# A two-layer encoder on one core: halves of x in two loads each, squares on two engines, constant products around the first norm, later places for means between the layers

## The chip, the cores and the metric

The kernel runs on one core of one Trainium2 chip. The metric is the device time of one execution in microseconds (us), the median of several runs. A core has a matrix engine (TensorE, PE in the profile; PEld is its loading of the stationary operand), a vector engine (VectorE, DVE), an engine for functions of one operand (ScalarE, ACT), a general one (GpSimd, POOL) and one that only issues transfers (SyncE, SP). Each works through its own queue in order and waits on semaphores. Matrix products are accumulated in PSUM, eight banks of 128 x 512 float32; everything else lies in SBUF.

## The reference

Two layers on x of 512 positions by 1024 channels, float32. All norms are RMS norms over the channels.

```
mem_n = rms_norm(mem, mem_norm_g)
for l in range(2):
    h = rms_norm(x, g_pre_mix[l])
    q_a, k_a, v_a, q_b, k_b, v_b, q_m, gate_pre = split(h @ w_in[l])
    o_a, o_b, o_m = neighbourhood(...), dilated(...), memory(q_m, mem_n @ w_mem_kv[l])
    merged = sum of sigmoid(gate_pre + b_gate[l]) * (o @ w_br)   # three branches
    x = x + rms_norm(merged @ w_out[l], g_post_mix[l])
    h = rms_norm(x, g_pre_ffn[l])
    u = depthwise_conv(h @ w_up[l], width 3)
    x = x + rms_norm((gelu(a) * b) @ w_down[l], g_post_ffn[l])   # a, b: halves of u
```

## The kernel before

Everything is held with channels on the 128 partitions and positions along the free side: x is eight tiles (index k) of 128 channels by 512 positions, worked in two halves of 256 positions. A product of full accuracy is made of three products: each operand is split into a high part (an ACT cast) and a low part (a subtraction on DVE or POOL), and `mm3` adds high by high, high by low and low by high. Weights come in blocks of 512 KB by SP (`weights`, line 226, three buffers `wraw`) and are split in the same way.

A norm needs the sum of squares over the channels, that is over partitions. ACT squares the tiles, DVE adds some of them, and `rstd_job` (line 325) lets PE multiply the sums as the stationary operand with a column of 1/1024 (`mean`): for each accumulator and each block of 128 positions one product of one column, which the trace records twice. ACT takes the square root, DVE the reciprocal, and two PE transposes spread the result over the partitions. In what follows "a mean" is these products, "the transposes" are the two of line 341.

The order of PE's instructions is written by a planner (`Woven`, line 46). It has a clock that each PE instruction advances by a planned cost (line 250: 0.107 us for three-part products of 256 columns, 0.213 for 512), and jobs, which are generators: `yield t` makes a job due t later by that clock, and it goes on at the first `tick` after that (`run_group` and `linear` tick after each k). `need(flag)` runs jobs until the flag is given. The planner does not measure; where a job's data are late on the chip, PE stands. The order on the other engines is set at build time by a scheduler that follows the order of the program as far as operands are ready in its own reckoning.

Three places matter here.

The start: `load_x` (line 192) brings the first half of x in four transfers of two tiles. Two constant products (`idle(2)`, line 883) run on PE meanwhile. `first_squares` (line 864) squares the eight tiles on ACT and adds them in pairs on DVE, so that the first half's mean has four accumulators; the second half's are added further, to two. `pre_norm_job` (line 363) does the norm: mean, root, reciprocal, transposes, then for each k a scaling on DVE, the high part on ACT, the low part on DVE. In between stand the splits of the first layer weights. The first projections need h of the first half (flag `h0.0.0`).

Between the layers: the last linear of layer 0 (`sublayer_end` with one tile, number 7, in halves) hands each half to a job. For the first half it is `end_job` (line 378): mean and transposes of the post-norm, then for each k a product, an addition into x, a square of the new x added to `acc2`; then `yield 9.0` (line 390) and the next layer's `pre_norm_job`, whose mean reads `acc2`. The second half goes through `raw_end_job` (line 417), which makes its own mean and, after `yield 3.5` (line 435), one over the new x. During this PE does the four memory projections of the next layer (`mem_kv`, line 478, 24 products of 256 columns each, every one into a new `mmbank` tile), and then the first pair of layer 1's projections for the first half.

Between mixing and channel mixing, in both layers: `factor_end_job` (line 393), once for each half, does the post-norm, adds into x, writes the not yet normalised h for the up-projection, squares, and after `yield 3.5` (line 409) takes the mean and copies the factor R. The first four up-projections run as a group over the halves (in two `sbank`, one `obank` and one `mmbank` tile); then come linears of 24 products of 512 columns, each in an `mmbank` tile. R is first read when the projections are read out (`scaled`, line 358).

```
131    ps_mm = ctx.enter_context(tc.tile_pool(name="ps_mm", bufs=3, space=bass.MemoryType.PSUM))
846                pss = [(sbank if SB and n0 == 0 and m % 2 else mmbank)((128, 256)) for m in pair]
482            ps = mmbank((128, N_MEM))
```

So full tiles, half tiles and memory projections share three buffers, and a new one waits until an old one has been read. The functions that the diff touches, and what calls them:

Of the kernel before, what the change touches and what calls it, by code (L numbers as in the profile page):

```python
# [9 lines left out]
AF = mybir.ActivationFunctionType  # L10
# [10 lines left out]
KD = D_MODEL // 128  # L21
# [4 lines left out]
HALVES = (slice(0, 256), slice(256, 512))  # L26
# [5 lines left out]
V_PRE, V_POST, V_PREF, V_POSTF, V_BG, V_CW, V_CB = 0, 8, 16, 24, 32, 56, 188  # L32
# [87 lines left out]
def tile_hybrid_encoder(ctx, tc, xT, memT, memg, vecs, rpb, w_in, w_kv, w_bra, w_brb, w_brm,  # L120
                        w_out, w_up, w_down, c_ident, c_mask, c_tab0, c_tab1, out):
    nc = tc.nc
# [14 lines left out]
    wv = Woven(tc)  # L137
# [12 lines left out]
    def ktile(dt=F32R, shape=(128, 512)):  # L150
        return tp.tile(list(shape), dt, tag="ka", name=nm("ka"), bufs=12)

    def ytile(shape=(128, 512)):
        return tp.tile(list(shape), F32, tag="y", name=nm("y"), bufs=8)
# [4 lines left out]
    def smalls(n=2):  # L159
        return sp.tile([128, n], F32, tag="st", name=nm("st"))  # L160
# [7 lines left out]
    def tbank(shape=(128, 512)):  # L168
        return ps_t.tile(list(shape), F32, tag="pt", name=nm("pt"))

    def obank(p=64):
        return ps_o.tile([p, 512], F32, tag="o", name=nm("o"))
# [5 lines left out]
    ACT, V = Counted(nc.scalar, wv, 0.1, 0.8e-3), Counted(nc.vector, wv, 0.065, 1.05e-3)  # L178
# [8 lines left out]
    xs = const.tile([128, 2, KD, 256], F32, name="x")  # L187

    def xh(k, half):
        return xs[:, half.start // 256, k, :]  # L190

    def load_x(half):
        for k in range(0, KD, 2):
            i = half.start // 256
            nc.sync.dma_start(out=xs[:, i, k:k + 2, :], in_=xT[:, i, k:k + 2, :])

    g0 = const.tile([128, KD], F32, name="g0")
    nc.scalar.dma_start(out=g0, in_=vecs[:, 0, V_PRE:V_PRE + KD])
# [46 lines left out]
    def mm(ps, a, b, first, last, cost):  # L245
        wv.pe(nc.tensor.matmul(ps, a, b, start=first, stop=last), cost)  # L246
# [66 lines left out]
    def sumsq_add(acc, src, first, slot=None, eng=None):  # L313
        if first:
            ACT.activation(acc, src, AF.Square)
        else:
            n = acc.shape[-1]
            sq = slot((128, 256)) if slot else small("sq2", 4) if n == 256 else small("sq", 1, (128, 512))
            ACT.activation(sq, src, AF.Square)
            (eng or V).tensor_add(acc, acc, sq)  # L320
# [1 line left out]
    def acctile():  # L322
        return small("acc", 2, (128, 512))

    def rstd_job(accs, n, box):

        nb = n // 128
        bank = tbank((128, n + nb))
        pr, pt = bank[:, 0:n], bank[:, n:n + nb]
        for i, a in enumerate(accs):  # L330
            for b in range(nb):
                mm(pt[:, b:b + 1], a[:, 128 * b:128 * b + 128], mean, i == 0 and b == 0,
                   i == len(accs) - 1 and b == nb - 1, 0.11)
        rs = smalls(nb)
        crit[0] = ACT.activation(rs, pt, AF.Sqrt, bias=eps, scale=1.0).ins
        V.reciprocal(rs, rs)
        yield 0.8
        for b in range(nb):
            one = rs[:, b:b + 1]
            spread = bass.AP(one.tensor, one.offset, [list(one.ap[0]), [0, 128]])  # L340
            wv.pe(nc.tensor.transpose(pr[:, 128 * b:128 * b + 128], spread, ident), 0.11)
        box.append(pr)

    def normed(src, g, rs, hi, lo, eng=None):
        h32 = small("h32", 3)
        V.scalar_tensor_tensor(out=h32, in0=src, scalar=g, in1=rs, op0=ALU.mult, op1=ALU.mult)
        split(h32, hi, lo, eng)

    def raw_split(l, goff, k, src, hi, lo):

        g = vec[:, l, goff + k:goff + k + 1]
        ACT.activation(hi, src, AF.Copy, scale=g)
        V.scalar_tensor_tensor(out=lo, in0=src, scalar=g, in1=f32(hi), op0=ALU.mult, op1=ALU.subtract)

    def rtile():
        return tp.tile([128, 512], F32, tag="R", name=nm("R"), bufs=1)
# [3 lines left out]
        V.tensor_mul(y, ps, R)  # L360
        return y

    def pre_norm_job(l, goff, acc, hs, i):
        half, box = HALVES[i], []
        yield from rstd_job(acc if isinstance(acc, list) else [acc[:, half]], 256, box)
        for k in range(KD):
            g = g0[:, k:k + 1] if l == 0 and goff == V_PRE else vec[:, l, goff + k:goff + k + 1]
            normed(xh(k, half), g, box[0], hs[k][0][:, half], hs[k][1][:, half],
                   G if k in LOG[l > 0 and goff == V_PRE] else V)
        crit[0] = last_copy[0]  # L370
        yield 1.2
        wv.give(f"h{l}.{goff}.{i}")
# [5 lines left out]
    def end_job(l, goff, og, acc, acc2, i, then, lat, more=()):  # L378
        half, box = HALVES[i], []
        yield lat  # L380
        yield from rstd_job([acc[:, half]] + list(more), 256, box)
        for k in range(KD):
            V.tensor_mul(og[k][:, half], og[k][:, half], box[0])
            (G if then is None and i and k in TAILG else V).tensor_add(xh(k, half), xh(k, half), og[k][:, half])
            if acc2 is not None:
                sumsq_add(acc2[:, half], xh(k, half), k == 0, None, G if k in SQG[goff == V_POSTF] else V)
            else:
                nc.sync.dma_start(out=out[:, k, half], in_=xh(k, half))
        if then is not None:
            yield 9.0  # L390
            yield from then(i)

    def factor_end_job(l, goff, og, acc, acc2, i, nxt):
# [23 lines left out]
    def raw_end_job(l, goff, og, acc, acc2, nxt, lat):  # L417


        half, box = HALVES[1], []  # L420
        hs, raw, R = nxt
        yield lat
        raw.extend((t[:, 0, :], t[:, 1, :]) for t in [ktile(F32R, (128, 2, 256)) for _ in range(KD)])
        yield from rstd_job([acc[:, half]], 256, box)
        for k in range(KD):
            V.tensor_mul(og[k][:, half], og[k][:, half], box[0])
            V.tensor_add(xh(k, half), xh(k, half), og[k][:, half])
            raw_split(l + 1, V_PRE, k, xh(k, half), *raw[k])
            if k == 0:
                yield 0.6  # L430
            wv.give(f"raw{k}")
            yield 1.05
        for k in range(KD):
            sumsq_add(acc2[:, half], xh(k, half), k == 0)
        yield 3.5
        box = []
        yield from rstd_job([acc2[:, half]], 256, box)
        ACT.copy(R[:, half], box[0])
        wv.give("R")
        for k in range(KD):  # L440
            normed(xh(k, half), vec[:, l + 1, V_PRE + k:V_PRE + k + 1], box[0], hs[k][0][:, half], hs[k][1][:, half])
        crit[0] = last_copy[0]
        yield 1.2
        wv.give(f"h{l + 1}.{V_PRE}.1")

    def h_tiles():
        return [(htile(), htile()) for _ in range(KD)]
# [46 lines left out]
    def group_weights(srcs, engs):  # L494
        return [weights(s, KD, 128, big, e) for s, e in zip(srcs, engs)]
# [368 lines left out]
    def first_squares(half):  # L864
        sqs = [ytile((128, 256)) for _ in range(KD)]
        for k in range(KD):
            ACT.activation(sqs[k], xh(k, half), AF.Square)
            if k % 2:
                V.tensor_add(sqs[k], sqs[k], sqs[k - 1])
            if k in (3, 5) and half != HALVES[0]:  # L870
                V.tensor_add(sqs[k], sqs[k], sqs[k - 2])
        return sqs[1::2] if half == HALVES[0] else sqs[5::2]

    idle_bank = obank(128)

    def idle(n):

        one, none = mean[:, 0:1], zero[:, 0:1]
        a, b = (bass.AP(t.tensor, t.offset, [list(t.ap[0]), [0, w]]) for t, w in ((one, 128), (none, 512)))
        for _ in range(n):  # L880
            mm(idle_bank, a, b, True, True, 0.0)

    idle(2)
    hs = h_tiles()
    wv.spawn(pre_norm_job(0, V_PRE, first_squares(HALVES[0]), hs, 0))
    gw = group_weights([w_in[0, m] for m in FIRST[:2]], (V, V))
    load_x(HALVES[1])
    nc.sync.dma_start(out=vec, in_=vecs)
    wv.need(f"h0.{V_PRE}.0")
    with tc.issue_after(last_copy[0]):  # L890
        sqs = first_squares(HALVES[1])
    wv.spawn(pre_norm_job(0, V_PRE, sqs, hs, 1), SD1)
    gw += group_weights([w_in[0, m] for m in FIRST[2:]], (V, G, V, G))
    for t, c in ((mask, c_mask), (tab0, c_tab0), (tab1, c_tab1)):
# [5 lines left out]
    for l in range(depth):  # L900
# [29 lines left out]
        acc = [None] * KD  # L930
# [20 lines left out]
        hs, R, gw = h_tiles(), rtile(), []  # L951
# [17 lines left out]
        for j in range(NFF):  # L969
            pair = []  # L970
            for m in (j, j + NFF):
# [3 lines left out]
                w = ahead.pop()  # L975
# [24 lines left out]
        else:  # L1000
            hm, km, vm = [], [], []
            wv.spawn(mem_norm_job(l + 1, hm, htile), 20.0)
            pre, R, raw, box = [], rtile(), [], []

            def then(a, i, l=l, box=box):
                box.extend(h_tiles())
                return pre_norm_job(l + 1, V_PRE, a, box, i)
# [21 lines left out]
            hs = box  # L1029
# [93 lines left out]
```

## Time and profile before

| | us |
|---|---|
| median of 3 runs (lowest to highest) | 1555.03 (1553.63 to 1556.48) |
| the profiled execution | 1552.91 |
| its span, first to last instruction | 1550.9 |
| PE busy | 1522.6 |
| DVE busy | 948.8 |
| ACT busy | 739.7 |
| POOL busy | 148.6 |

A timeline row reads: start, duration from the first start to the last end, engine, line, operation, tile written <- tiles read, shape, number of instructions, and in brackets how long the engine was idle before and what released it. L114 is a helper that issues for ACT and DVE, L246 the one for products, so rows are told apart by their tiles: `x` the stream, `y` and `sq` squares and scratch, `acc` sums of squares, `pt` the bank of a mean, `mm`, `s`, `o` banks of products, `st` the small root, `h` and `ka` operands, `m`, `whi`, `wlo` split weights and other large tiles. "PE pt <- DVE acc" in the waits is total time, number of times, longest. A row of a table by stretches has, after the stretch and its length, busy time and instructions of PE, PEld, DVE, ACT and POOL, the granted clock of PE as a share, the share of the transfer engines and their GB/s. The profile gives a granted clock of 1.00 until its first record of the clock, also where products run at half the pace.

### The profile page before, as it was taken

What the parts mean: (1) busy time and instruction counts of PE and PEld (TensorE: products, weight loads), DVE (VectorE), ACT (ScalarE), POOL (GpSimd) and SP (SyncE); (2) the same over time, 40 slices, a digit from 0 to 9 for tenths busy, and PEclk for the clock granted to TensorE, in tenths of its full rate; (3) what the DMA queues carried; (4) which work ended last, traced back from release to release, by engine and by line L of the source; (5) the groups of instructions that cost most, each with busy time, mean ns of one, the idle gap of its engine ahead of it and who ended that gap; (6) DMA issues with size and microseconds to landing.
All of it is one profiled execution on the core that took longest, in us unless ns stands there. A gap on an engine that the chain in (4) does not pass through costs nothing.

```text
span 1550.9 us, 20677 instructions
## 1 busy us (share of the span) xinstructions
PE 1522.6 (98%) x7970; PEld 1300.1 (84%) x7970; DVE 948.8 (61%) x1684; ACT 739.7 (48%) x1288; POOL 148.6 (10%) x216
## 2 busy tenths in 40 slices
PE   8999999999999999999989999999999999999997
PEld 7988878888988888888888888888889888888887
DVE  6685666335777777743397856753456977776233
ACT  6465575235544444533355556742354544444231
POOL 3340000210000000010154300002100000000000
PEclk9999999999999999999999999999999999999998
DMA  7221113234112332333431221132350223233331
GB/s 246 91 90 61 61 57 98 93 95 157 61 55 96 99 104 96 108 96 102 129 103 59 79 69 58 52 109 88 102 177 15 82 96 98 102 99 89 98 105 62
DMA packets 45810, 144.91 MB, mean 93 GB/s; under 512 B 5376, under 2 KB 9600, under 8 KB 45712
## 3 DMA queue, kind: packets, MB, share of 16 engines
q1 hardware_dynamic: 43776, 139.85, 28.0%
q10 hardware_dynamic: 1296, 2.10, 0.4%
q0 software_dynamic: 640, 1.64, 0.4%
q8 instruction: 62, 1.02, 0.3%
q14 instruction: 36, 0.29, 0.1%
HBM read 141.48 MB, written 2.10 MB: 93 GB/s over the span
## 4 chain that ended last, share of the span: by engine, by line
PE 91%; DVE 5%; ACT 2%; DMA 1%; issue 1%; SPq 0%; ACTq 0%; DVEq 0%
PE mm L246 80%; PE s L246 4%; PE o L246 3%; PE pt L257 2%; DVE y L114 1%; DVE m L114 1%; PE pt L246 1%; DVE x L114 1%; DVE ka L114 1%; DVE acc L114 1%; ACT y L114 0%; DMA vec<-in_vecs_dram 0%; DVE wlo L114 0%; ACT m L114 0%; ACT whi L114 0%
## 5 line engine op out<-in xcount | busy, mean ns | idle before, releaser
L246 PE MATMUL mm<-h,whi 128*128 128x512 f32 x2496 | 775.5, 392 | 0.0
L246 PEld LDWEIGHTS mm<-h,whi 128*128 128x128 f32 x2496 | 461.4, 188 | 90.9
L246 PE MATMUL mm<-h,wlo 128*128 128x512 f32 x1248 | 486.3, 390 | 0.0
L114 DVE TENSOR_TENSOR wlo<-wraw,whi 128x1024 fp32r<-128x1024 f32 (+1 forms) x213 | 259.1, 1217 | 284.2 <-ACT whi L114 281.4
L114 ACT CAST whi<-wraw 128x1024 fp32r<-128x1024 f32 (+1 forms) x213 | 221.1, 1038 | 305.8 <-PE mm L246 292.0
L246 PEld LDWEIGHTS mm<-h,wlo 128*128 128x128 f32 x1248 | 234.3, 188 | 49.6
L246 PE MATMUL mm<-m,whi 128*128 128x512 f32 (+1 forms) x800 | 215.1, 356 | 0.9 <-DVE m L114 0.8
L246 PEld LDWEIGHTS mm<-m,whi 128*128 128x128 f32 x800 | 141.8, 189 | 22.8 <-PE mm L246 1.3
L246 PE MATMUL mm<-m,wlo 128*128 128x512 f32 (+1 forms) x400 | 142.2, 355 | 0.0
L114 DVE SCALAR_TENSOR_TENSOR y<-y,vec,y 128x511 f32<-128x511 f32 x176 | 130.4, 747 | 3.5 <-ACT y L114 0.9
L114 DVE TENSOR_TENSOR y<-mm,R 128x512 f32<-128x512 f32 x82 | 56.3, 687 | 68.4 <-PE mm L246 68.4
L246 PEld LDWEIGHTS mm<-m,wlo 128*128 128x128 f32 x400 | 75.5, 189 | 10.9
L801 POOL TENSOR_TENSOR m<-m,y 128x512 f32<-128x512 f32 x28 | 36.0, 1287 | 402.4 <-DVE y L114 402.4
L114 ACT ACTIVATE y<-y,vec 128x512 f32<-128x512 f32 x88 | 70.9, 813 | 2.1 <-DVE y L114 1.9
L246 PE MATMUL mm<-m,m 128*128 128x512 f32 x240 | 63.6, 395 | 0.0
L114 ACT ACTIVATE y<-y 128x512 f32<-128x512 f32 x44 | 27.8, 632 | 72.3 <-DVE y L114 71.9
L114 DVE TENSOR_TENSOR acc<-acc,sq 128x256 f32<-128x256 f32 (+1 forms) x80 | 41.0, 513 | 27.3 <-ACT sq L114 25.4
L114 ACT CAST m<-pt 128x512 fp32r<-128x512 f32 (+1 forms) x72 | 38.4, 540 | 40.5 <-PE pt L257 31.8
L114 ACT ACTIVATE y<-mm,vec 128x512 f32<-128x512 f32 (+1 forms) x91 | 57.4, 630 | 0.1
L114 DVE TENSOR_TENSOR m<-pt,m 128x512 fp32r<-128x512 f32 (+1 forms) x72 | 44.9, 629 | 18.8 <-ACT m L114 17.9
L114 ACT ACTIVATE y<-y,st 128x256 f32<-128x256 f32 (+1 forms) x80 | 43.7, 547 | 26.7 <-DVE st L114 26.6
L114 ACT CAST m<-y 128x512 fp32r<-128x512 f32 x32 | 19.8, 619 | 72.5 <-DVE y L114 72.5
(152 smaller groups left out, 1808.6 us busy)
## 6 DMA issues: line engine op xcount, KB each, us to landing
wraw<-in_w_in_dram SPq DMA_DIRECT2D x88, 512.0 KB, 3.7
wraw<-in_w_up_dram SPq DMA_DIRECT2D x88, 512.0 KB, 3.6
wraw<-in_w_down_dram SPq DMA_DIRECT2D x32, 512.0 KB, 3.5
wraw<-in_w_out_dram SPq DMA_DIRECT2D x16, 512.0 KB, 4.2
wraw<-in_w_down_dram SPq DMA_DIRECT2D x16, 384.0 KB, 3.1
wraw<-in_w_kv_dram SPq DMA_DIRECT2D x8, 512.0 KB, 4.1
wraw<-in_w_bra_dram SPq DMA_DIRECT2D x16, 192.0 KB, 2.3
x<-in_xT_dram SPq DMA_DIRECT2D x8, 256.0 KB, 5.9
```

Of the source, the lines that this page charges most:

```text
L114: return op(*args, **kw)
L246: wv.pe(nc.tensor.matmul(ps, a, b, start=first, stop=last), cost)
L257: wv.pe(nc.tensor.transpose(ps[:, 128 * i:128 * i + 128], s, ident), 0.11)
L801: (V if br == 2 and m >= 6 else G).tensor_add(acc[m], acc[m], gs)
```

## The change

Four edits. (1) `load_x` brings each half of x in two transfers of four tiles (512 KB) in place of four of two tiles. (2) In the first half's squares, tiles 3, 6 and 7 are squared on DVE, the other five on ACT; tiles 0 and 1, and 2 and 3, are still added, tiles 4 to 7 not, so that the mean takes six accumulators, in the order 1, 3, 4, 7, 5, 6. (3) `idle` can take fewer columns, and the first norm calls it: one constant product of 256 columns between its mean and its transposes, two behind the transposes. (4) The mean of the next layer's norm for the first half is due 12.5 after the additions into x in place of 9.0, and the means of the middle norm, in both layers and for both halves, 5.0 after the squares in place of 3.5.

```
     def load_x(half):
-        for k in range(0, KD, 2):
+        for k in range(0, KD, 4):
             i = half.start // 256
-            nc.sync.dma_start(out=xs[:, i, k:k + 2, :], in_=xT[:, i, k:k + 2, :])
+            nc.sync.dma_start(out=xs[:, i, k:k + 4, :], in_=xT[:, i, k:k + 4, :])
...
-    def rstd_job(accs, n, box):
+    def rstd_job(accs, n, box, warm=None):
...
         V.reciprocal(rs, rs)
+        if warm:
+            warm(1, 256)
         yield 0.8
...
             wv.pe(nc.tensor.transpose(pr[:, 128 * b:128 * b + 128], spread, ident), 0.11)
+        if warm:
+            warm(2, 256)
         box.append(pr)
...
         if then is not None:
-            yield 9.0
+            yield 12.5
             yield from then(i)
...
             sumsq_add(acc2[:, half], xh(k, half), k == 0)
-        yield 3.5
+        yield 5.0
         box = []
...
         for k in range(KD):
-            ACT.activation(sqs[k], xh(k, half), AF.Square)
-            if k % 2:
+            if half == HALVES[0] and k in (3, 6, 7):
+                V.tensor_mul(sqs[k], xh(k, half), xh(k, half))
+            else:
+                ACT.activation(sqs[k], xh(k, half), AF.Square)
+            if k % 2 and (k < 4 or half != HALVES[0]):
                 V.tensor_add(sqs[k], sqs[k], sqs[k - 1])
             if k in (3, 5) and half != HALVES[0]:
                 V.tensor_add(sqs[k], sqs[k], sqs[k - 2])
-        return sqs[1::2] if half == HALVES[0] else sqs[5::2]
+        return [sqs[k] for k in (1, 3, 4, 7, 5, 6)] if half == HALVES[0] else sqs[5::2]
...
-    def idle(n):
+    def idle(n, w=512):
...
         for _ in range(n):
-            mm(idle_bank, a, b, True, True, 0.0)
+            mm(idle_bank[:, 0:w], a, b, True, True, 0.0)
...
-    wv.spawn(pre_norm_job(0, V_PRE, first_squares(HALVES[0]), hs, 0))
+    wv.spawn(pre_norm_job(0, V_PRE, first_squares(HALVES[0]), hs, 0, idle))
```

The constant products have a planned cost of 0 and move nothing in the planner; the two more accumulators add 0.44 to its clock.

More of the change, by code (lines that the diff above doesn't have):

```diff
@@ L361, in scaled, with pre_norm_job @@
         return y
-    def pre_norm_job(l, goff, acc, hs, i):
+    def pre_norm_job(l, goff, acc, hs, i, warm=None):
         half, box = HALVES[i], []
-        yield from rstd_job(acc if isinstance(acc, list) else [acc[:, half]], 256, box)
+        yield from rstd_job(acc if isinstance(acc, list) else [acc[:, half]], 256, box, warm)
         for k in range(KD):
@@ L871, in first_squares @@
                 V.tensor_add(sqs[k], sqs[k], sqs[k - 2])
-        return sqs[1::2] if half == HALVES[0] else sqs[5::2]
+        return [sqs[k] for k in (1, 3, 4, 7, 5, 6)] if half == HALVES[0] else sqs[5::2]
     idle_bank = obank(128)
-    def idle(n):
+    def idle(n, w=512):
         one, none = mean[:, 0:1], zero[:, 0:1]
-        a, b = (bass.AP(t.tensor, t.offset, [list(t.ap[0]), [0, w]]) for t, w in ((one, 128), (none, 512)))
+        a, b = (bass.AP(t.tensor, t.offset, [list(t.ap[0]), [0, w]]) for t, w in ((one, 128), (none, w)))
         for _ in range(n):
-            mm(idle_bank, a, b, True, True, 0.0)
+            mm(idle_bank[:, 0:w], a, b, True, True, 0.0)
     idle(2)
     hs = h_tiles()
-    wv.spawn(pre_norm_job(0, V_PRE, first_squares(HALVES[0]), hs, 0))
+    wv.spawn(pre_norm_job(0, V_PRE, first_squares(HALVES[0]), hs, 0, idle))
     gw = group_weights([w_in[0, m] for m in FIRST[:2]], (V, V))
```

## The prediction

> **What bounds the kernel now.** I read the page first (busy shares, chain), then who the tensor engine (PE) waits for, then the three stretches that the diff touches, engine by engine in order of time.
>
> ```profile
> span 1550.9 us, 20677 instructions
> PE 1522.6 (98%) x7970; PEld 1300.1 (84%) x7970; DVE 948.8 (61%) x1684; ACT 739.7 (48%) x1288; POOL 148.6 (10%) x216
> ...
> PE 91%; DVE 5%; ACT 2%; DMA 1%; issue 1%; SPq 0%; ACTq 0%; DVEq 0%
> ```
>
> PE is busy for 98% and the chain runs over it for 91%. So a time counts if it moves the end of PE's work: PE's idle stretches, and places where PE would have to wait after the change. What PE waits for longest:
>
> ```profile
> PE pt L246 <- DVE acc L114: 4.6, 2, 3.4
> ...
> PE pt L246 <- DVE y L114: 2.4, 2, 1.4
> ```
>
> The first row is two means between the layers (3.4 and 1.2 us), the second the two means of the first norm. These are the edit's places. All sums below are made against the profiled execution, 1552.91 us (span 1550.9 and 2.0 around it); the median shown, 1555.03, is 2.1 above it, and I add the change to that median. A change of 0.2% is 3.1 us, about what a measurement of this kernel can tell from none.
>
> **Part 1, the start: loads, squares, constant products.**
>
> ```profile
> 0.98 3.78 PE L246 MATMUL o<-zero,mean 128*128 128x512 f32 x4 [0.98 <-POOL zero L206]
> ...
> 6.43 1.44 ACT L114 ACTIVATE y<-x 128x256 f32<-128x256 f32 x4 [1.39 <-DMA x<-in_xT_dram]
> ...
> 7.67 1.87 PE L246 MATMUL pt<-mean,y 128*128 128x1 f32 x8 [1.01 <-DVE y L114]
> 7.91 0.42 DVE L114 TENSOR_TENSOR y<-y,y 128x256 f32<-128x256 f32 x1 [0.30 <-ACT y L114]
> 9.57 0.26 ACT L114 ACTIVATE st<-pt,eps 128x2 f32<-128x2 f32 x1 [1.69 <-PE pt L246]
> 9.73 1.12 ACT L114 CAST m<-wraw 128x512 fp32r<-128x512 f32 x2
> ...
> 10.08 0.69 PE L341 MATMUL pt<-ident,st 128*128 128x128 f32 x2 [0.55 <-DVE st L114]
> 10.81 0.48 DVE L114 SCALAR_TENSOR_TENSOR h<-x,g,pt 128x256 f32<-128x256 f32 x1 [0.78 <-DMA x<-in_xT_dram]
> ...
> 21.90 1.05 PE L246 MATMUL pt<-mean,y 128*128 128x1 f32 x8 [1.40 <-DVE y L114]
> ```
>
> The last squares start when x lands, 6.43. A summed pair of tiles costs PE two column blocks of two records each, so the eight records at 7.67 are the last two of four accumulators. They end at 9.54, and the square root starts at once. Afterwards the accumulators are six, and the four that come from the second transfer are not summed in pairs: sixteen records behind the landing in place of eight. Eight take 1.87 here, sixteen about 3.7.
>
> When does the second transfer land? It carries what the third and fourth do now. The chain of waits has the third:
>
> ```profile
> 1.19 0.42 SPq L195
> ...
> 1.66 4.75 DMA x<-in_xT_dram
> ```
>
> It lands at 6.41; the fourth is in by about 7.1, since the four squares from 6.43 run on without a break (1.44). The new second transfer is issued in the second place (1.19, 0.47 sooner than the third), so it lands between 5.9 and 7.1; I take 6.6. The first square is 0.4 later, sixteen records 3.7 more: 10.7 against 9.54, plus 1.2 (from 0.5 to 1.7). The dropped additions and the shared squares save 0.42 and some squares ahead of PE, but PE's own queue of records is what ends last. The clock in these rows is the closed one: the eight records take 1.87 at 7.67 and 1.05 at 21.90, although products had run for 3.78 from 0.98 on. The Trainium skill, "TensorE: Matmul & The Clock Gate", Part 1, has the clock open after about 3.4 us of sustained products; by that, the sixteen would take 2.1, the start would cost nothing, and the sum would be plus 3.3 in place of plus 4.7. The row at 7.67 speaks against it, so I go by the row and keep the other as rival C.
>
> The constant products: four records of 512 columns take 3.78, so one product of 256 (two records) takes 0.95 at this rate. It stands in the 0.54 between mean and transposes, and can push the transposes by 0.4 at most, by 0 if the root comes later; I take 0.2, since half the gap remains after the records overlap. The two products behind the transposes (1.9) end before the second product of the first pair can start, as that one waits for DVE until 13.28; cost 0.
>
> So the first normalisation on DVE (10.81) moves by 1.4. It is on the path:
>
> ```profile
> 11.00:14.00 3.00, 1.30 (x4) 1.01 (x5) 3.00 (x7) 1.85 (x4) 0.00 (x0) 1.00 0.86 326
> 14.00:19.70 5.70, 5.61 (x35) 5.31 (x34) 5.70 (x16) 3.63 (x10) 0.00 (x0) 1.00 0.91 309
> ```
>
> The third pair of figures is DVE: full from 11 to 19.7. PE then idles 1.40 at 21.90 for the second half's squares, which come behind that. Nothing is free there to take up the 1.4. Bounds: plus 1.9 with the late landing; minus 0.8 if ACT does the first weights' casts (now at 9.73, behind the root) ahead of it, for then up to 2.2 us of DVE's weight subtractions could leave the stretch. The order of the two ACT rows speaks for the late end. I take **plus 1.4**. Four SP issues of x go, and the weights behind them are issued earlier, but their casts wait for the root anyway.
>
> **Part 2, the mean between the layers (9.0 to 12.5).** PE, ACT and DVE rows:
>
> ```profile
> 778.49 3.04 PE L246 MATMUL mm<-h,m 128*128 128x256 f32 x24
> 784.97 0.64 PE L246 MATMUL pt<-mean,acc 128*128 128x1 f32 x4 [3.44 <-DVE acc L114]
> 785.47 2.27 PE L246 MATMUL mm<-h,m 128*128 128x256 f32 x9
> ```
> ```profile
> 783.95 0.42 ACT L114 ACTIVATE sq<-x 128x256 f32<-128x256 f32 x1 [0.59 <-DVE x L114]
> 784.27 0.36 ACT L114 ACTIVATE sq<-mm 128x256 f32<-128x256 f32 x1
> 784.53 0.47 ACT L114 ACTIVATE y<-mm,vec 128x256 f32<-128x256 f32 x1
> ...
> 788.20 1.26 DVE L114 SCALAR_TENSOR_TENSOR h<-x,vec,pt 128x256 f32<-128x256 f32 x3 [0.34 <-PE pt L341]
> ```
> ```profile
> 814.83 0.58 PE L246 MATMUL pt<-mean,acc 128*128 128x1 f32 x4 [1.16 <-DVE acc L114]
> ```
>
> PE has done the second memory projection (24 products, from 778.49) and idles 3.44 for the mean. The planner counts 0.107 us for a 256-column product, so 3.5 later are 33 products: the mean goes behind the third projection and the third step of the fourth. But the third projection needs a buffer of the three that mmbank has (line 131). In turn they go to tile 6, the first half of tile 7, its second half, projections 0, 1, 2: projection 2 takes the buffer of tile 7's second half. ACT reads that at 784.27 and 784.53, behind the last square of x, and is done at 785.00. So PE stands until 785.0 all the same, for another release: **gain 0.0**, where the mean's end at 785.4 comes 0.4 later than the buffer, and the mean's own 0.44 is paid later.
>
> What moves is the normalisation behind it. PE gets to the transposes 33 products later, 4.2 us at 3.04 per 24, so DVE starts at 792.4 in place of 788.2. PE is through the projections at about 793.1 (48 products from 785.4, 18 of them at the half clock below, and two transposes). DVE does three rows first (1.26) and then the low part of the first h (0.4), so that PE's second product of the next layer finds its operand at 794.1 and waits up to 1.0; I take 0.7. DVE then gives one k per two operations of under 0.4, PE takes one per six products of 0.12: nothing is made up. Further on DVE is the bound of the row at 814.83:
>
> ```profile
> 788.20:796.00 7.80, 7.80 (x66) 7.80 (x66) 7.03 (x19) 4.99 (x14) 0.42 (x2) 0.96 0.01 3
> 796.00:814.70 18.70, 17.67 (x148) 17.40 (x146) 17.78 (x36) 10.20 (x24) 11.77 (x18) 1.00 0.38 128
> ```
>
> Of these 26.5 us DVE is idle for 1.7. Started 4.2 later, it ends up to 2.5 later, unless weight subtractions fill 787.9 to 792.4. So this part costs between 0.1 (all filled) and 2.9; I take **plus 1.5**, the 0.7 and half of what is left.
>
> The clock here:
>
> ```profile
> 781.40:785.00 3.60, 0.16 (x3) 0.07 (x1) 3.39 (x8) 1.80 (x6) 0.83 (x1) 1.00 0.64 209
> 785.40:788.80 3.40, 3.40 (x18) 3.40 (x18) 2.24 (x7) 1.35 (x5) 3.03 (x8) 0.51 0.00 1
> 788.80:792.20 3.40, 3.40 (x30) 3.40 (x30) 2.91 (x9) 1.97 (x6) 0.00 (x0) 1.00 0.02 5
> ```
>
> After 3.4 us without products, PE runs 3.4 us at 0.51, 18 products in place of 30: 1.4 us. As the idle time stays, this cost stays.
>
> **Part 3, the means of the middle norm (3.5 to 5.0), in both layers.** No mean there has an idle time ahead of it, so nothing is gained. What is paid:
>
> ```profile
> 434.61 0.50 PE L246 MATMUL pt<-mean,acc 128*128 128x1 f32 x4
> ...
> 440.08 0.61 PE L246 MATMUL mm<-h,whi 128*128 128x512 f32 x2
> ...
> 440.76 0.61 PE L246 MATMUL mm<-h,whi 128*128 128x512 f32 x2
> ...
> 446.20 0.61 PE L246 MATMUL mm<-h,whi 128*128 128x512 f32 x2
> ```
> ```profile
> 437.27 1.29 DVE L114 TENSOR_TENSOR y<-s,R 128x512 f32<-128x512 f32 x2 [1.65 <-ACT R L114]
> ...
> 445.04 0.68 DVE L114 TENSOR_TENSOR y<-mm,R 128x512 f32<-128x512 f32 x1
> ```
>
> The second half's mean stands right behind its group. By the due times (its squares are written five steps into the group of eight, 3.84 ahead of the group's end by the planner) 1.5 later falls behind the second step of the next linear, 0.68 each in the rows 440.08 and 440.76: 1.36 later. R comes 1.36 later, and DVE, which waits for R at 437.27, starts at 438.6. Its work up to the row at 445.04 has no break, so that row ends at 447.1 in place of 445.72. It releases the mm buffer of the fourth tile of the group, and the linear at 446.20 is the fourth to ask for one: slack now 0.48, then a wait of 0.9. In layer 1 the same rows:
>
> ```profile
> 1209.86 0.68 DVE L114 TENSOR_TENSOR y<-mm,R 128x512 f32<-128x512 f32 x1
> ...
> 1211.03 0.62 PE L246 MATMUL mm<-h,whi 128*128 128x512 f32 x2
> ```
>
> Twice 0.9 is **plus 1.8**; from 0 (DVE's order changes) to 2.7 (the slack used up elsewhere too). The first half's means cost nothing: nobody waits for that half of R alone.
>
> **Sum:** 1.4 + 1.5 + 1.8 = plus 4.7: 1557.6 on the profiled execution, 1559.7 on the median.
>
> **Rivals.** A: the buffer of projection 2 is free earlier, and the idle 3.44 goes, with the 1.4 of the half clock. For it: the trace can name only the later of two waits. Against it: the ACT order above. Even then PE meets DVE at the row of 814.83: the normalisation starts 1.0 sooner, and of DVE's 1.7 idle at most all goes, so 1.0 to 2.7 is left of 4.8; with minus 1.9 in place of the plus 1.5 the sum is plus 1.3, 1556.3, no change that can be told. It decides from the point at which ACT's read of tile 7 precedes the square row of 783.95. B: DVE's order in part 3 changes, so that the release comes first: plus 2.9, 1557.9. C: the constant products open the clock earlier. The eight records at 21.90 take 1.05 against 1.87 at 7.67, so the sixteen would take 2.1, the start would cost 0 instead of 1.4: plus 3.3, 1558.3. For it: sixteen records and the products keep PE without a gap. Against it: the new products stand behind the mean, and the opening ones, unchanged, did not do it. D: ACT casts ahead of the root, the start gains 0.8: plus 2.5, 1557.5. That the moved means do not move is no case: lines 390 and 409 set due times that no flag forces earlier there.
>
> **How the numbers follow.** The forecast has 0.45, A 0.2, B 0.12, C 0.08, D 0.05, several of them at once 0.1. Low: A at 2.7, part 3 free and D, minus 3.5, 1551.5. High: 1.9 + 2.7 + 2.9, 1562.5. The forecast's bounds put 0.37 of its 0.45 above 3.1 us, B, C and D half of their 0.25: slower 0.49. Same is 0.08 of the forecast, the other half of B, C and D, and 0.16 of A: 0.36. Faster is the best of A, 0.04, and the several at once: about 0.15.
>
> **What would show it.** Right: the square root of the first norm at about 10.7; PE idle from 781.4 to 785.0, now ahead of a projection product and released by ACT; DVE's h rows from about 792.4, and more than 1.16 idle at the later mean; PE idle about 0.9 near 446 and 1211. Wrong: no idle time near 781; a root before 9.5; no wait near 446. The first would make it a gain, the last two take 3.3 away.

## The result, and the profile after

| | us |
|---|---|
| before, median of 12 runs | 1553.87 |
| after, median of 12 runs | 1556.86 |
| ratio after to before | 1.0018, 95% interval 1.0009 to 1.0026 |
| the same in us | plus 2.8, interval 1.4 to 4.0 |
| profiled execution after | 1554.37, span 1552.3 |

The change makes the kernel a little slower, in the direction of the forecast and with less than its plus 4.7. (Single executions far longer than the rest, here one of the kernel after at a granted clock of 0.65, are left out of every ratio; without it the median after is 1556.44.)

First the page of the kernel after: span, busy time, the chain that ended last.

```profile
span 1552.3 us, 20685 instructions
...
PE 1525.1 (98%) x7984; PEld 1301.5 (84%) x7984; DVE 949.8 (61%) x1685; ACT 739.9 (48%) x1285; POOL 150.1 (10%) x216
...
PE 92%; DVE 5%; ACT 2%; issue 1%; DMA 0%; ACTq 0%
```

The span is only 1.4 longer, and PE is still the whole story. Then what PE waited for, in the kernel after (total time, times, longest):

```profile
PE mm L246 <- ACT y L114: 3.6, 1, 3.6
...
PE pt L343 <- ACT m L114: 2.1, 1, 2.1
PE pt L246 <- DVE y L114: 2.0, 2, 1.0
```

The row "PE pt <- DVE acc" of before (4.6 in two waits) is gone. In its place stand a product that waits 3.6 for an ACT read, and 2.1 at two transposes. Where these are, the timeline of the kernel after shows:

```profile
776.63 3.04 PE L246 MATMUL mm<-h,m 128*128 128x256 f32 x24
783.22 5.47 PE L246 MATMUL mm<-h,m 128*128 128x256 f32 x33 [3.55 <-ACT y L114]
...
790.33 0.48 DVE L114 SCALAR_TENSOR_TENSOR h<-x,vec,pt 128x256 f32<-128x256 f32 x1 [0.80 <-PE pt L343]
...
791.92 2.05 PE L246 MATMUL mm<-h,m 128*128 128x256 f32 x11 [0.23 <-DVE h L114]
...
794.57 0.27 ACT L114 ACTIVATE st<-pt,eps 128x2 f32<-128x2 f32 x1 [0.84 <-PE pt L246]
...
797.90 0.16 DVE L114 RECIPROCAL st<-st 128x2 f32<-128x2 f32 x1
798.20 0.40 PE L343 MATMUL pt<-ident,st 128*128 128x128 f32 x2 [2.13 <-ACT m L114]
...
816.38 0.50 PE L246 MATMUL pt<-mean,acc 128*128 128x1 f32 x4
```

The first row is the second memory projection, 1.86 sooner than before (776.63 against 778.49). Behind it PE stands 3.55, and now the third projection waits, for an ACT read of `y`. The mean and its normalisation come later (first h row 790.33). The row 797.90 is the new loss: the reciprocal of the second half's norm, whose root was there at 794.84, is queued on DVE behind all h rows of the first half, and PE waits 2.13 for the transposes that need it. (The bracket of the row 798.20 names an ACT cast, but the transposes read no tile that it writes; they read `st`, which the reciprocal has written by 798.06, 0.14 ahead of them. No run moved this reciprocal, so this cause is read from the trace alone.) The last row, the later mean, has no idle time ahead of it any more; before, it had 1.16.

The start, in the timeline of the kernel after:

```profile
5.71 3.35 PE L246 MATMUL pt<-mean,y 128*128 128x1 f32 x24 [1.04 <-DVE y L114]
...
9.09 0.26 ACT L114 ACTIVATE st<-pt,eps 128x2 f32<-128x2 f32 x1 [2.64 <-PE pt L246]
...
21.68 1.05 PE L246 MATMUL pt<-mean,y 128*128 128x1 f32 x8 [0.99 <-DVE y L114]
```

The twenty-four records take 3.35 and not twenty-four times 0.213: they stand 0.112 apart until the granted clock falls to a half at 7.86, and the last four 0.213 apart; the root starts at 9.09 (before 9.57), the second half's mean at 21.68 (before 21.90). This start is 0.2 faster.

The two profiles can't be subtracted as they stand, though, for the clock fell differently. Stretches behind an idle time, first of the kernel before, then of the kernel after (PE's busy time and products, four more engines, granted clock, transfers):

```profile
24.20:27.60 3.40, 3.40 (x18) 3.40 (x17) 2.49 (x6) 1.99 (x6) 0.97 (x1) 0.50 0.73 241
...
874.10:877.50 3.40, 3.13 (x18) 2.69 (x19) 1.85 (x3) 2.53 (x4) 2.39 (x5) 1.00 0.00 0
```
```profile
24.20:27.60 3.40, 3.40 (x31) 3.40 (x30) 3.07 (x8) 2.31 (x5) 1.26 (x2) 1.00 0.72 254
...
874.80:878.20 3.40, 3.40 (x13) 2.72 (x12) 1.92 (x2) 2.12 (x3) 1.37 (x4) 0.51 0.00 0
```

Before, the clock is halved at 24 and open at 874; after, it is the other way round. Each halved stretch of 3.4 costs 1.7. The same two waits in both, one near 60 and one near 939, each first before and then after:

```profile
61.56 0.47 PE L246 MATMUL mm<-m,whi 128*128 128x256 f32 x2 [0.84 <-DVE m L114]
...
937.91 0.71 PE L246 MATMUL s<-m,m 128*128 128x128 f32 x4 [0.45 <-DVE st L114]
```
```profile
59.84 0.47 PE L246 MATMUL mm<-m,whi 128*128 128x256 f32 x2 [0.85 <-DVE m L114]
...
939.45 0.71 PE L246 MATMUL s<-m,m 128*128 128x128 f32 x4 [0.45 <-DVE st L114]
```

The kernel after is 0.2 ahead at the second mean, 1.7 ahead at 60, level at 830 (the same products start at 830.46 and 830.42), and 1.5 behind at 939. So the middle costs 1.8, and the clock gives 1.5 and takes 1.5, by chance in one execution each.

### The profile page after: what moved, and what is told of

The parts are those of the page before. It is cut to its first block, busy times and chain, and to the rows that moved or that the text cites. A ratio compares the mean times of both kernels' runs of the same rounds, so it can differ in the third digit from the quotient of the medians.

```text
span 1552.3 us, 20685 instructions
## 1 busy us (share of the span) xinstructions
PE 1525.1 (98%) x7984; PEld 1301.5 (84%) x7984; DVE 949.8 (61%) x1685; ACT 739.9 (48%) x1285; POOL 150.1 (10%) x216
## 4 chain that ended last, share of the span: by engine, by line
PE 92%; DVE 5%; ACT 2%; issue 1%; DMA 0%; ACTq 0%
PE mm L246 80%; PE s L246 5%; PE o L246 4%; PE pt L257 2%; PE pt L246 1%; DVE m L114 1%; DVE y L114 1%; DVE h L114 1%; DVE x L114 0%; DVE wlo L114 0%; DVE ka L114 0%; ACT y L114 0%; ACT whi L114 0%; ACT m L114 0%; PE pt L343 0%
## 5 line engine op out<-in xcount | busy, mean ns | idle before, releaser
L246 PEld LDWEIGHTS mm<-m,wlo 128*128 128x128 f32 x400 | 75.5, 189 | 10.8
L246 PE MATMUL mm<-h,m 128*128 128x256 f32 x312 | 50.0, 303 | 4.5 <-ACT y L114 3.6
```

## The experiments

Twelve kernels, each compared with the kernel before on the same chip. "In us" is the ratio times that kernel's median (1554.1 to 1554.3).

| run | what it is | ratio, 95% interval | in us |
|---|---|---|---|
| start_all | start edits alone | 1.0005, 0.9997 to 1.0014 | +0.8 |
| first_mean | 9.0 to 12.5 alone | 1.0012, 1.0003 to 1.0022 | +1.9 |
| later_mean | 3.5 to 5.0 at line 435 alone | 0.9986, 0.9977 to 0.9995 | -2.2 |
| both_means | both of these | 1.0009, 0.9998 to 1.0020 | +1.4 |
| mid_norm | 3.5 to 5.0 at line 409 instead | 1.0011, 1.0001 to 1.0020 | +1.7 |
| kv_bank | both means, one projection in an s bank | 0.9983, 0.9975 to 0.9992 | -2.6 |
| kv_bank11 | the same with 11.0 for 12.5 | 1.0001, 0.9991 to 1.0011 | +0.2 |
| loads_only | larger loads alone | 0.9996, 0.9987 to 1.0006 | -0.6 |
| cold_six | new loads and squares, no constant products | 1.0015, 1.0006 to 1.0024 | +2.3 |
| cold_pairs | new loads, squares in pairs, no constant products | 0.9997, 0.9985 to 1.0010 | -0.5 |
| after_kv | whole change, s bank | 0.9978, 0.9968 to 0.9989 | -3.4 |
| kv_loads | kv_bank and larger loads | 0.9975, 0.9965 to 0.9985 | -3.9 |

**A misreading comes first.** The prediction and the text ahead of it put the second delay, 3.5 to 5.0, into `factor_end_job` (line 409). The diff's lines stand in `raw_end_job` (line 435): the two functions hold the same lines around the `yield`, and only the hunk's line number tells them apart. Between mixing and channel mixing nothing is changed. What is moved is the mean of the second half between the layers, which is the row at 814.83 of before; it goes two steps later, behind 30 products of its linear in place of 18. The experiments take the edit where it stands, and mid_norm takes it where it was priced.

**The change in parts.** start_all:

> The kernel before with the three edits at the start alone (loads, squares, constant products). Theory of the prediction: the sixteen mean records behind the second landing go at 0.21 each, the root of the first norm comes at about 10.7 in place of 9.57, and the kernel is slower by 1.4 us. Rival, from the profile after: the second transfer lands at 5.7 and not at 6.6, and what the records cost depends on whether the clock is open, which changes from execution to execution; root between 9.1 and 10.8, the whole between 0.2 us faster and 1.1 us slower.

Measured plus 0.8 (minus 0.5 to plus 2.2), not to be told from nothing. Its profile, timeline:

```profile
5.47 2.84 PE L246 MATMUL pt<-mean,y 128*128 128x1 f32 x24 [0.72 <-DVE y L114]
...
8.35 0.26 ACT L114 ACTIVATE st<-pt,eps 128x2 f32<-128x2 f32 x1 [2.06 <-PE pt L246]
```

Here all records go at 0.112 and the root comes 1.2 sooner than before, sooner also than either theory had it, though the median is not lower: one profile is one draw, as the runs on the records below show.

first_mean:

```
-            yield 9.0
+            yield 12.5
```

> The kernel before with the 9.0 to 12.5 alone. Theory: this edit makes the loss. The idle 3.4 stays, ahead of a projection product; the normalisation on DVE comes 3.9 us later against PE, so that PE idles about 2 us for the transposes of the second half's mean and still some for the later mean: slower by 1.8 to 2.1 us. Prediction on record: 1.5 us. Rival: the loss in the profile after lies in the clock and at the start, and this edit costs nothing (within 0.5 us).

Measured plus 1.9. The timeline of its PE waits in this place:

```profile
785.09 5.73 PE L246 MATMUL mm<-h,m 128*128 128x256 f32 x33 [3.54 <-ACT y L114]
794.05 2.04 PE L246 MATMUL mm<-h,m 128*128 128x256 f32 x11 [0.23 <-DVE h L114]
800.32 0.40 PE L341 MATMUL pt<-ident,st 128*128 128x128 f32 x2 [2.13 <-ACT m L114]
818.27 0.58 PE L246 MATMUL pt<-mean,acc 128*128 128x1 f32 x4 [1.03 <-DVE acc L114]
```

The 3.5 stays, 0.23 and 2.13 are new, and 1.03 of the 1.16 is left at the later mean: in all 2.3 more idle time than before, where the runs measured 1.9. This edit makes the loss.

later_mean:

> The kernel before with the 3.5 to 5.0 of the second half between the layers alone (line 435), the mean two steps of twelve products in all later. Theory: the idle 1.16 us ahead of this mean goes and nothing is late for it: faster by 1.2 us. Rival, as the prediction had it for its misplaced edit: R comes later and a reader of R keeps a bank, so that PE waits elsewhere: 0 to 1 us slower.

Measured minus 2.2 (interval minus 3.6 to minus 0.8). Its timeline, the first mean and the later one:

```profile
784.15 0.99 PE L246 MATMUL pt<-mean,acc 128*128 128x1 f32 x4 [3.47 <-DVE acc L114]
...
815.33 0.50 PE L246 MATMUL pt<-mean,acc 128*128 128x1 f32 x4
```

No idle time is left ahead of the later mean, and nothing else became late. The trace accounts for 1.2 of the gain, which the interval holds.

both_means:

> The kernel before with both means between the layers moved, the start as before. Theory: the sum of the two, where the later mean takes back only the idle time that is left to it: slower by 1.4 to 1.8 us, nearly all of the change's loss. Rival: the means together cost nothing and the loss of the whole change comes from the start: within 0.5 us.

Measured plus 1.4, with an interval that takes in nothing as well as the expected 1.8. Its trace has the same waits as the change (3.54, 0.23, 2.12, none at the later mean): 1.3 more idle time than before. With the 0.8 of start_all that makes 2.2 of the change's 2.8.

**Is it the buffer?** The prediction said that the 3.4 stays because projection 2 needs an mm buffer that ACT reads last. kv_bank, beside both means:

```
-            ps = mmbank((128, N_MEM))
+            ps = (sbank if pre and m == 2 else mmbank)((128, N_MEM))
```

> The kernel before with both means between the layers moved, and the third memory projection of layer 1 in a bank of the s pool in place of the mm pool. Theory of the prediction's part 2: the idle 3.5 us stayed because this projection waited for the mm buffer that ACT reads last; with another bank PE goes on at once, the idle falls below 1 us, the clock is not halved behind it (1.4 to 1.7 us), the mean and all behind it come up to 3.5 us sooner: 2 to 4 us faster than with both means alone, so 0 to 2 us faster than the kernel before. Rival: the wait is for something else that comes as late (operands on DVE), the idle stays at 3.5 and the time is that of both means, 1.8 us slower than before.

Measured minus 2.6, 4.0 below both_means by the ratios. Timeline, and the stretch behind it (columns as above):

```profile
780.22 3.04 PE L246 MATMUL s<-h,m 128*128 128x256 f32 x24
783.93 1.34 PE L246 MATMUL mm<-h,m 128*128 128x256 f32 x9 [0.67 <-ACT y L114]
...
795.41 0.41 PE L341 MATMUL pt<-ident,st 128*128 128x128 f32 x2 [2.13 <-ACT m L114]
```
```profile
785.00:788.80 3.80, 3.49 (x27) 2.90 (x25) 2.67 (x8) 2.21 (x7) 2.31 (x7) 1.00 0.02 4
```

The third projection (first row) follows the second without a break; the fourth now takes that buffer and waits 0.67 for the same ACT read. The idle 3.5 is gone and the clock stays open. So the buffer it was: against both_means PE's idle time between 776 and 832 falls from 5.9 to 3.3, a halved stretch worth 1.7 goes, and of these 4.3 the runs show 4.0. The 2.13 at the transposes is untouched. What this does not show is that the first mean is better off at its later place. later_mean leaves it where it was, keeps the mm buffer and measures minus 2.2; the 0.4 between the two lie far within the intervals.

> As the run with the s bank, but the mean of the first half due after 11.0 in place of 12.5, so that it stands inside the third projection. Theory: PE idles about 1.4 for the sum of squares in place of 3.4, the clock stays open, and the normalisation starts as early as in the kernel before: 1 to 3 us faster than the kernel before, more than with 12.5. Rival: DVE sets the pace from the first normalisation to the later mean, what PE gains at 781 it loses at the first pair of layer 1: within 0.5 us of the kernel with the later mean alone, 1.2 to 2.1 faster than before.

Measured plus 0.2: by the median neither theory, as it gains nothing, though the interval (minus 1.4 to plus 1.7) still holds the low end of both. In its profile PE waits 1.31 ahead of the mean, 1.40 and 1.82 ahead of the two pairs of transposes, and the clock is halved twice (from 788.8 and from 799.0). An early mean puts its chain of root, reciprocal and transposes back onto PE's path. How much of it each wait makes was not taken further.

**The mechanism priced in the wrong place.** mid_norm:

> The kernel before with 3.5 to 5.0 at line 409 alone, the means of the middle norm in both layers, which is the place that the prediction priced and that the change does not touch. Prediction's mechanism: R 1.36 us later, the read of the fourth bank 1.36 later, PE idle 0.9 near 446 and near 1211: 1.8 us slower. Rival: DVE takes other work first and the bank is read in time: no idle there, within 0.3 us.

Measured plus 1.7. Timeline of DVE, then of PE in both layers:

```profile
438.41 1.29 DVE L114 TENSOR_TENSOR y<-s,R 128x512 f32<-128x512 f32 x2 [1.67 <-ACT R L114]
...
445.92 0.68 DVE L114 TENSOR_TENSOR y<-mm,R 128x512 f32<-128x512 f32 x1
...
446.75 0.70 PE L246 MATMUL mm<-h,whi 128*128 128x512 f32 x2 [0.57 <-DVE y L114]
...
1215.00 0.70 PE L246 MATMUL mm<-h,whi 128*128 128x512 f32 x2 [0.57 <-DVE y L114]
```

These times have to be read against PE's own work, which runs a little sooner in this execution. The last row of the group, before and in mid_norm:

```profile
434.25 0.52 PE L246 MATMUL mm<-h,m 128*128 128x256 f32 x3
```
```profile
434.00 0.52 PE L246 MATMUL mm<-h,m 128*128 128x256 f32 x3
```

With this 0.25 added, R comes 1.4 later (438.41 against 437.27), as the two steps say, and the read of the fourth bank 1.1 later (445.92 against 445.04): DVE made up some 0.25. PE waits at the very linear that was named, in both layers. That linear starts 0.8 later (446.75 against 446.20, and the 0.25); the bracket shows 0.57 of it, as it counts from the modelled end of products that overlap. The working had 0.9, and twice 0.8 is 1.6 of the 1.7 measured.

**The start.** loads_only and kv_loads:

> The kernel before with the two larger transfers for each half of x alone; squares in pairs and eight mean records behind the last landing as before. Theory: the second transfer lands at about 5.6, where the fourth landed at 7.1, and the root comes at 8.3 to 8.5 in place of 9.57: 1.1 us faster. Rival, as the prediction had it: the landing stays near 6.6 or the gain is swallowed by the clock: 0 to 0.5 us faster.

> Both means moved, the s bank, and the two larger transfers, with the squares in pairs as before and no more constant products. Theory: the landing at 5.6 to 5.9 brings the root to 8.4 to 9.3, on top of the run with the s bank alone: 2.5 to 3.7 us faster than the kernel before. Rival: what comes earlier at the start is waited for at the second half's mean, about 20 us on: the same as with the s bank alone, 2.5 faster.

loads_only measured minus 0.6, not to be told from nothing. kv_loads measured minus 3.9, the lowest ratio here, but its lead over kv_bank, 1.2, lies within the intervals. loads_only, timeline:

```profile
5.83 2.48 PE L246 MATMUL pt<-mean,y 128*128 128x1 f32 x16 [1.07 <-DVE y L114]
...
8.35 0.26 ACT L114 ACTIVATE st<-pt,eps 128x2 f32<-128x2 f32 x1 [0.44 <-PE pt L246]
...
17.98 3.41 DVE L114 TENSOR_TENSOR y<-y,y 128x256 f32<-128x256 f32 x6
...
19.78 2.73 POOL L224 TENSOR_TENSOR m<-wraw,m 128x512 fp32r<-128x512 f32 x2 [13.96 <-ACT m L114]
```

The root comes 1.2 sooner, as the theory had it, but the second half's mean ends its wait at 21.44, only 0.5 sooner than before: the six additions ahead of it take 3.41, where before they took 2.53, and a subtraction on POOL now runs beside the last of them.

cold_six and cold_pairs take the constant products out, so that the clock can't open before the mean:

> The new loads and the new squares (six accumulators, twenty-four records) without any constant product, so that no window of the clock can open before the mean. Leaves out work that enters no output. Prediction's mechanism: twenty-four records at 0.213, sixteen of them behind the second landing, root at 10.6 to 10.8. Rival: records do not depend on the products ahead of them; root at 8.4 to 9.1 as in the profiles with the whole start.

> The new loads with the squares in pairs as before (sixteen records, eight behind the last additions), and no constant product either. Prediction's mechanism: root at 9.2 to 9.5, 1.2 to 1.5 before that of the six accumulators, and the whole faster than that one by about as much. Rival: equal roots, since squares and additions and not records end last.

Timelines of cold_six, of cold_pairs, and of after_kv, which has the whole start of the change:

```profile
5.85 5.25 PE L246 MATMUL pt<-mean,y 128*128 128x1 f32 x24 [5.85 <-DVE y L114]
...
11.14 0.26 ACT L114 ACTIVATE st<-pt,eps 128x2 f32<-128x2 f32 x1 [4.64 <-PE pt L246]
```
```profile
5.84 3.54 PE L246 MATMUL pt<-mean,y 128*128 128x1 f32 x16 [5.84 <-DVE y L114]
...
9.42 0.26 ACT L114 ACTIVATE st<-pt,eps 128x2 f32<-128x2 f32 x1 [1.53 <-PE pt L246]
```
```profile
5.53 5.28 PE L246 MATMUL pt<-mean,y 128*128 128x1 f32 x24 [0.78 <-DVE y L114]
...
10.85 0.27 ACT L114 ACTIVATE st<-pt,eps 128x2 f32<-128x2 f32 x1 [4.56 <-PE pt L246]
```

With a closed clock eight more records cost 1.7 (11.14 against 9.42), which is eight times 0.213, where 1.2 to 1.5 was expected; both sets of records start only at 5.85, and so the first root comes later than its 10.6 to 10.8. The whole is slower by 2.8 (plus 2.3 against minus 0.5), and the intervals hold the 1.7. The third profile is a draw of the change's own start with a closed clock: root at 10.85. So the same start gives a root at 8.35, 9.09 or 10.85, by the clock of that execution.

> The whole change, and the third memory projection in a bank of the s pool. Theory: the start costs and gains about as much (0 to 1 us slower than the same kernel with the start as before), so 1.5 to 2.5 us faster than the kernel before; the only thing in the change that loses is the mm buffer. Rival: the start makes a good part of the loss, 1.5 us or more, and this run is level with the kernel before.

Measured minus 3.4: the whole change with one bank moved is faster than the kernel before, and not slower than kv_bank. With the start the pair of means is 1.4 slower (the change against both_means), with start and bank 0.8 faster (after_kv against kv_bank): the signs differ, and both lie within the intervals, so the start as a whole neither costs nor gains anything that these runs can tell.

## Why the prediction was right in direction, and which steps failed

**Start, plus 1.4.** Measured plus 0.8 alone (minus 0.5 to plus 2.2), and nothing visible between after_kv and kv_bank. Two steps failed and cancelled, which is luck. The second transfer lands at 5.5 to 5.8 in every profile with the larger loads, not at 6.6 and outside the bounds of 5.9 to 7.1. And not sixteen but all twenty-four records lie behind it: the first transfer carries four tiles and lands at 4.2 to 4.5, so that the first sum is ready only at 5.5. From there 24 times 0.213 and what follows give the 10.85 measured, where the working had 10.7. The third failed step is the clock: that the opening products "did not do it" was read from one execution. Rival C, an open clock, was given 0.08 and held wholly in one and for the most part in another of the three profiles that have this start. Yet it is not the work of the new products: the clock opens at 4.4 to 5.4, before they run, and three profiles with the start of before have it too (both_means, later_mean, kv_bank).

**Mean between the layers, plus 1.5.** Right, and the reason too: PE stands as long as before, released by ACT's last read, and kv_bank shows that it is this buffer. The half clock stayed. The first h row is 13.7 behind the start of the second projection, where it was 9.7 (788.20 less 778.49): 4.0 later, forecast 4.2. The size was about right (plus 1.9 measured alone), its place not: 0.2 in place of 0.7 at the first pair, and the rest not at the later mean but at the second half's transposes, whose reciprocal stands in DVE's queue behind the h rows. The prediction asked who waits for the first half's norm, not what else was in DVE's queue.

**Middle norm, plus 1.8.** Wrong, by reading the wrong function. The real edit gains: 1.2 of idle time alone, 1.0 in company with the other delay. The mechanism was sound where it was priced: plus 1.7 measured against 1.8, with 0.8 in each layer seen in the trace.

**Sum.** Read rightly, the same working would have given 1.4 and 1.5 less some 1.0, plus 1.9; the change measured plus 2.8, 1.4 to 4.0. The forecast of 4.7 was too high by the misplaced term. Two of its own signs of being wrong came in, a root before 9.5 in two profiles of three and no wait near 446; by its word they take away 3.3. That the direction held is due to the one part that was read rightly, the first mean; that the total stayed near the measured 2.8 owes much to luck. Of the rivals, A (buffer free) is refuted by the 3.55 that stayed, B has no place in the change (and in mid_norm the waits came), D did not show: the root comes ahead of the casts in all three profiles with this start.

## What to carry to other kernels

Before moving work that seems late, find out what the next instruction in the queue is waiting for: here a buffer came free at nearly the same time as the sum, and with another buffer the same moves took 4.0 less. Compare also with leaving the work where it was: the gain that is left over that (0.4) could not be told from none. Of a step that comes later, list everything behind it in the same engine's queue, other chains' small steps above all. And read a diff by its hunk's lines against the file, not by text that stands there twice; a fraction of a percent is judged from many executions, as two profiles can differ by 3 us through the clock alone.

## What was not expected of the hardware

**The clock.** In each trace the records of the granted clock stand at multiples of 3.413 us from one another, but where the first one falls in the span differs from execution to execution. Of the twelve profiles with constant products at the start, seven have the clock open from 4.4 to 5.4 on and five only from 16.5 to 19.8, with the same work. At the wait near 874, windows that hold 1.93 to 2.17 us of idle time were followed by a halved clock, in eight profiles; in six, with 1.83 or less in one window, it stayed open, though in two of these the whole wait was 2.0 and 2.1, cut by the end of a window. Elsewhere idle time alone does not decide: windows with 1.66 and 1.82 (kv_bank11) were followed by a halved clock, others with 1.85 to 1.92 (after_kv, kv_bank) were not. Nor does a busy PE keep the clock open: in start_all the window from 5.41 holds 0.06 of idle time, PE working mainly on the one-column products of the mean, and the clock was halved from 8.83. The Trainium skill, "TensorE: Matmul & The Clock Gate", Part 1, describes a free-running window of 3413 ns whose place varies from run to run; the traces agree. It gives a whole idle window as the condition for closing; here 1.9 of 3.4 was enough, so on this the measurement decides.

**Two engines on one addition.** In loads_only the last of the six DVE additions takes 1.49 in place of 0.42: it starts at 19.90, 0.12 behind a POOL subtraction of 1.32 and ends 0.28 after it. The Trainium skill, "SBUF — State Buffer", section "SBUF: two separate sides", says that a DVE operation with two SBUF inputs and a GpSimd operation that reads SBUF take a shared port in turn, each for its whole length. The trace agrees.

**Fewer, larger loads.** The same 1 MB of x is in at 5.5 to 5.8 as two transfers of 512 KB (seven profiles), and at 6.8 to 8.0 as four of 256 KB (seven).
